# Head forms through eight staging slots, an x-sum loaded later, and a re-timed end of the gated-convolution units, in a streaming hybrid layer

## The chip, the cores and the metric

The kernel runs on one core of one Trainium2 chip. The metric is device time in microseconds (us) of that core. TensorE is called PE here, VectorE DVE, ScalarE ACT, GpSimd POOL and SyncE SP; PEld is PE's loading of weights, which runs beside its matmuls.

## The reference

One layer of a streaming encoder is computed for 512 prompt frames of a new stream and 64 frames of a running one (with 512 cached keys and values). All inputs and outputs are float32.

```
D_MODEL 2048; 8 heads x 128; 8 conv groups x 128 channels, width 3; D_FF 5632; IN_COLS 6144
def hybrid_layer(x, ...):
    hn = rmsnorm(x, g_norm1)
    q, k, v, gb, gc, hc = split(hn @ w_in)            # six times 1024 columns
    q, k = rmsnorm(q, g_q), rmsnorm(k, g_k)           # per head
    o_attn = stick_breaking_blocks(q, k_all, v_all, P).reshape(B, T, 1024)
    u = gc * hc
    conv = conv_w[0]*padded[:, 0:T] + conv_w[1]*padded[:, 1:T+1] + conv_w[2]*padded[:, 2:T+2]
    o_conv = gb * conv                                # padded = past state, then u
    mix = concatenate([rmsnorm(o_attn, g_attn_out), rmsnorm(o_conv, g_conv_out)])
    x = x + mix @ w_out
    h2 = rmsnorm(x, g_norm2)
    x = x + (silu(h2 @ w_gate) * (h2 @ w_up)) @ w_down
```

New keys, values and conv states are outputs too.

## The kernel before

**Layout and precision.** Features lie on the 128 partitions and frames in the free dimension: 512 + 64 = 576 frames, worked in two halves of 288 (`HALVES`). A float32 operand is split into a rounded high part (a cast on ACT, line 223 in `split`) and the remainder as a low part (a subtraction on DVE, or on POOL where `lo_eng` says so, line 224). A product is three matmuls: high by high, low weight by high, high weight by low. One "tick" of the software pipeline `pipe` is one such group of three matmuls; generators that yield a number of ticks are put into the instruction streams between them.

**Stages.** First come norms, q/k/v projections and attention, head by head, then two conv groups in the plain way (`conv_group`, `STD` = 2). The other six conv groups, and the attention half of the output projection, are computed in units of a 2x2 block scheme that needs seven products (numbers 1 to 7, with sums of weights and sums of inputs) in place of eight. There are 17 units: n = 0 to 8 are conv units (lists `CU`, `NCU` = 9; kind "u" makes u = gc * hc of a group, kind "b" the gate of two groups), n = 9 to 16 are output units (kind "o"), one for each 256 output columns. A product of a conv unit has 24 matmuls, one of an output unit 12. After the units comes the plain output projection of the conv half (`out_proj`, bank name `pjo`), which starts at 855.88 us of the profile, then the second norm and the feed-forward part to the end.

**Order of the units.** PE runs the products in a list written out by hand, `corder` (lines 1089 to 1097); `conv_run` issues one product and the work on its bank, and `conv_prepare`, four places ahead in the list, forms the weight sum of a later product on DVE and splits it (`whl`, two tags in turn). The raw columns of w_in and w_out lie in three places, which `call_columns` fills when they fall free: 0 and 1 (`raw_a`, 1 MB each) and 2 (`bt["raw"]`, named `raw_c`); output units use 0 and 1 alone. Except for PE, the order on each engine is the scheduler's; from product 1 of the last conv unit on, SP's too is the order in which the code is written, for as long as `turn_mode` is open (lines 1100 to 1117).

**Inputs of the products.** In a conv unit products 5, 6, 7 and 4 read sums of x blocks. Sum 0 lies in `xt` (loaded by the eight DMAs of line 1085), sums 1, 2 and 3 in tiles `xs_t1` to `xs_t3` of 2.3 MB each (tags t1 to t3), all three loaded in `open_b` when attention ends. Product 6 reads sum 1, product 7 sum 2, product 4 sum 3, product 5 sum 0. In an output unit the seven inputs are "forms" of the normed heads. `head_forms` makes them: a sum of squares over the heads, the row scale `acc_a`, then for each of four head pairs two scalings on DVE, the three forms 1, 2, 3, which are blocks, and four forms 5, 7, 6, 4, which POOL makes by subtraction. `put` splits each into a tile `hf` and stores it to `form_dram` by SP (line 542): 28 forms, 288 KB each. The tile comes from tag "hl" of the pool `tmp`, with two buffers, which `put_mix` and the squares of `group_scale` use as well. `load_forms` fetches the forms into tags t1, t2, t3 and "oa" during the last conv unit (lines 1108 to 1114), as the products that read the old contents end.

**The last conv unit and the output units.** The order of unit 8 is 1, (unit 7's 3 and 4), 6, 7, 5, 4, 2, 3. After product 5 the bank `psw` is read by DVE (`done`, lines 1003 to 1007, name `cv`), and product 4 adds to the same bank. After product 3 `open_out` opens tiles for the residual (16 loads `x` from `xt_dram`, one for each 128 rows, all issued at once on SP) and for `mixc`, the normed conv outputs that `put_mix` had written to `mix_dram`; `load_mix` asks for its two halves at ticks 60 and 120. `group_scale` makes the row scale `R_c` of the conv half: squares split at once, their sums on PE 40 ticks later (`ssg`), `rsqrt_mean` (lines 457 to 466: `ms` on DVE, logarithm and exponential on ACT, three DVE steps with `y` and `t`), then the second half of the frames in the same way 80 ticks after the start. `ms` has one buffer, and `kept("ms")`, the copy of product 1's bank (`part`, line 991), has the same tag. The eight output units hold 8 x 28 = 224 ticks. The first two weights of `out_proj` are loaded at the tenth and fifth product before the end of `corder`.

Of the kernel before, what the change touches and what calls it, by code (L numbers as in the profile page):

```python
# [10 lines left out]
F32 = mybir.dt.float32  # L11
F32R = mybir.dt.float32r
# [4 lines left out]
P = 128  # L17
TP = 512
TS = 64
T = TP + TS  # L20
HALF = T // 2
# [13 lines left out]
NP = KD // 2  # L35
# [59 lines left out]
def tile_hybrid_stream_step(  # L95
# [6 lines left out]
    nc = tc.nc  # L102
# [13 lines left out]
    rpool = ctx.enter_context(tc.tile_pool(name="rpool", bufs=1, side="left"))  # L116
# [92 lines left out]
    pipe = Pipeline()  # L209
# [16 lines left out]
    def parts(name):  # L226
        t = tmp.tile([P, 2, HALF], F32R, tag="hl", name=name)
        return t[:, 0], t[:, 1]
# [290 lines left out]
    def head_forms():  # L519

        two = [parts("sqg") for _ in HALVES]
        for (sh, sl), (a, b) in zip(two, HALVES):
            split(sh, sl, acc_a[:, a:b])
        yield 6
        for (sh, sl), (a, b) in zip(two, HALVES):
            rsqrt_mean(acc_a[:, a:b], channel_sums(sh, sl, a, b, "ssg"), 8 * P, HALF)
        yield 8
        for k in range(NH // 2):  # L530
            pair = o_half[k // 2][:, 2 * (k % 2) : 2 * (k % 2) + 2, :]
            four = pair.rearrange("p k (i t) -> p (k i) t", i=2)
            b11, b12, b21, b22 = (four[:, q, :] for q in range(4))
            for r in range(2):
                nc.vector.scalar_tensor_tensor(out=pair[:, r], in0=pair[:, r], scalar=col("ga", 2 * k + r), in1=acc_a,
                                               op0=ALU.mult, op1=ALU.mult)
            yield 2

            def put(f, src, lo_eng):
                t = tmp.tile([P, 2, HALF], F32R, tag="hl", name="hf")  # L540
                split(t[:, 0], t[:, 1], src, lo_eng)
                nc.sync.dma_start(out=form_dram[f - 1, k].rearrange("f p t -> p f t"), in_=t.bitcast(F32))

            for f, src in ((1, b11), (2, b21), (3, b22)):
                put(f, src, nc.vector)
                yield 2
            for f, out, a, b in ((5, b11, b12, b11), (7, b12, b12, b22), (6, b22, b22, b11), (4, b21, b21, b22)):
                nc.gpsimd.tensor_tensor(out=out, in0=a, in1=b, op=ALU.subtract)
                yield 1
                put(f, out, nc.gpsimd if f in (5, 6) else nc.vector)  # L550
                yield 2

    def group_scale(acc, dst, rows_of):

# [273 lines left out]
    def open_b():  # L828

        pipe.flush()  # L830
        t1.release()
        bt["pool"] = bpool = tc.alloc_tile_pool(name="bpool", bufs=1, reuse_waits="tile", side="left")
        for q in (1, 2, 3):
            t = bt[q] = bpool.tile([P, NP, 2, HALF], F32R, tag=f"t{q}", name=f"xs_t{q}")
            nc.sync.dma_start(out=t.bitcast(F32), in_=xs_dram[q].rearrange("j f p t -> p j f t"))
        bt["acc"] = acon.tile([P, T], F32, tag="ac", name="acc_c")
        pipe.spawn(head_forms(), 2)

    def open_units():
        bt["raw"] = apool.tile([P, 2048], F32, tag="oa", name="raw_c")  # L840
        cx = apool.tile([P, 1024 + UW], F32, tag="ob", name="cx")
        bt["s1"] = cx[:, :1024].rearrange("p (j c) -> p j c", c=P)
        bt["c"] = cx[:, 1024 : 1024 + UW - 2]
# [36 lines left out]
    def conv_group(g):  # L880
        gates = []

        def evac_gc(ps, a, b):
            t = tmp.tile([P, HALF], F32, tag="sq", name="gcr")
            nc.vector.tensor_tensor(out=t, in0=ps, in1=R1[:, a:b], op=ALU.mult)
            nc.vector.tensor_tensor(out=t, in0=t, in1=R1[:, a:b], op=ALU.mult)
            gates.append(t)

        project(evac_gc)
        begin_u(g)  # L890
        project(lambda ps, a, b: put_u(a, b, ps, gates[a // HALF]))

        def evac_gb(ps, a, b):
            if not bt:
                open_b()
            if a == 0:
                end_u(g)
            t = tmp.tile([P, HALF], F32, tag="y", name="gbr")
            nc.vector.tensor_tensor(out=t, in0=ps, in1=R1[:, a:b], op=ALU.mult)
            put_o(g, a // HALF, t)  # L900

        if g == STD - 1:
            call_columns(range(2))
            for p_ in (1, 2):
                conv_prepare(0, p_)
        project(evac_gb)
# [11 lines left out]
    def call_columns(gone):  # L918
        cfree.extend(gone)
        while cwanted:  # L920
            n, c = cwanted[0]
            place = [q for q in cfree if c is not None or q < 2][:1]
            if not place:
                return
            cwanted.pop(0)
            q = place[0]
            cfree.remove(q)
            raw = bt["raw"] if q == 2 else raw_tile["A"][:, q, :]
            if c is None:
                d = CU[n][1]  # L930
                nc.sync.dma_start(out=raw.rearrange("p (k c) -> p k c", c=2 * P),
                                  in_=w_out[:AW, 2 * d * P : 2 * (d + 1) * P].rearrange("(k p) c -> p k c", p=P))
                v = raw.rearrange("p (j s h c) -> p j s h c", s=2, h=2, c=P)
                for c in range(2):
                    cregion[n, c] = q, v[:, :, 0, c, :], v[:, :, 1, c, :]
            else:
                c0 = cstart[c + 2 * (CU[n][0] == "b")] + CU[n][1] * P
                nc.sync.dma_start(out=raw.rearrange("p (k c) -> p k c", c=P),
                                  in_=w_in[:, c0 : c0 + P].rearrange("(k p) c -> p k c", p=P))
                v = raw.rearrange("p (j s c) -> p j s c", s=2, c=P)  # L940
                cregion[n, c] = q, v[:, :, 0, :], v[:, :, 1, :]
# [106 lines left out]
    def open_out():  # L1048

        xpool.release()  # L1050
        bt["y"] = ypool = tc.alloc_tile_pool(name="ypool", bufs=1, reuse_waits="tile", side="right")
        x2t.extend(ypool.tile([P, 2, T], F32, tag=f"y{j}", name=f"x2_{j}") for j in range(NP))
        bt["m"] = tc.alloc_tile_pool(name="mpool", bufs=1, reuse_waits="tile", side="right")
        bt["mc"] = bt["m"].tile([P, 2, NG, 2, HALF], F32R, name="mixc")
        for kt in range(KD):
            nc.sync.dma_start(out=x2(kt), in_=xt_dram[kt])
        bt["R"] = rpool.tile([P, T], F32, tag="R", name="R_c", bufs=2)
        pipe.spawn(state_out())
        pipe.spawn(group_scale(bt["acc"], bt["R"], 40))
        pipe.spawn(load_mix())  # L1060

    def load_mix():
        for i in range(2):
            yield 60
            nc.sync.dma_start(out=bt["mc"][:, i].bitcast(F32), in_=mix_dram[i].rearrange("k f p t -> p k f t"))

    def state_out():
# [17 lines left out]
        nc.sync.dma_start(out=xt[j][:, 0, 1].bitcast(F32), in_=xs_dram[0, j].rearrange("f p t -> p f t"))  # L1085
    pipe.flush()
    open_units()
    call_columns([2])
    corder = [(0, 1), (0, 2), (1, 1), (1, 2), (0, 6), (0, 7), (0, 5), (0, 3), (0, 4), (1, 6), (1, 7), (1, 5)]
    for n in range(2, len(CU)):  # L1090
        if n == NCU - 1:
            corder += [(n, 1), (n - 1, 3), (n - 1, 4), (n, 6), (n, 7), (n, 5), (n, 4), (n, 2), (n, 3)]
        elif n == NCU:
            corder += [(n, p_) for p_ in (1, 2, 6, 7, 5)]
        else:
            corder += [(n, 1), (n - 1, 3), (n - 1, 4), (n, 2), (n, 6), (n, 7), (n, 5)]
# [4 lines left out]
    for k_, (n, p_) in enumerate(corder):  # L1101
        if (n, p_) == (NCU - 1, 1):
            turn_mode.enter_context(tc.manual_schedule(engines={mybir.EngineType.SP}))
        conv_run(n, p_)
        if k_ + 4 < len(corder):
            conv_prepare(*corder[k_ + 4])
        if n == NCU - 1 and p_ in (6, 7, 4):
            q = {6: 1, 7: 2, 4: 3}[p_]
            t = bt["pool"].tile([P, NH, 2, HALF], F32R, tag=f"t{q}", name=f"forms{q}")
            for at, f in enumerate({1: (1, 2), 2: (6, 7), 3: (5, 3)}[q]):  # L1110
                load_forms(t, 4 * at, f)
            if p_ == 7:
                load_forms(apool.tile([P, NH // 2, 2, HALF], F32R, tag="oa", name="forms0"), 0, 4)
        if (n, p_) == (NCU - 1, 3):
            open_out()
            turn_mode.close()
        if k_ in (len(corder) - 10, len(corder) - 5):
            load_weight()
        if k_ == len(corder) - 4:
            split_weight(nc.vector)  # L1120


    ypool, mpool, mc, R_c = (bt[n] for n in ("y", "m", "mc", "R"))
# [616 lines left out]
```

## Time and profile before

| what | value |
|---|---|
| median of 3 runs | 2456.91 us (2456.89 to 2457.04) |
| profiled execution, its own time | 2452.86 us |
| span of the profile | 2451.1 us |
| mean granted clock of PE | 0.99 |
| PE / PEld busy | 2383.6 (97%) / 2368.5 (97%) us |
| DVE / ACT / POOL busy | 1903.9 (78%) / 1168.5 (48%) / 290.4 (12%) us |
| DMA | 386.05 MB, mean 157 GB/s |
| first matmul of the first unit | 504.58 us |
| first matmul of `out_proj` | 855.88 us |

The profile shows one execution. Busy time counts an engine's own work and not its waiting; SP's DMA issues appear as a queue (SPq). In lists of groups and in timelines an entry reads "output<-input", with "L982" for line 982 of the kernel, and in brackets the idle time of the engine before it and what ended that. Times in timelines and windows are us from the start of the span, on which attention and the two plain conv groups end at about 504 us.

### The profile page before, as it was taken

Reading aid. Unit: us, or ns where it says so; the run is one execution under the profiler, and the core shown is the slowest. Engines: PE = TensorE matmul, PEld = TensorE weight load, DVE = VectorE, ACT = ScalarE, POOL = GpSimd, SP = SyncE. Lnnn points to the kernel's source line nnn. Section 1 sums busy time; section 2 is a strip of 40 time slices with the busy share of each in tenths; the row PEclk is TensorE's granted clock in tenths of the full one; section 3 lists DMA queues with packets and bytes.
Section 4 is the critical chain, followed back from the end, with each engine's and each line's share of the span. In section 5 each row is a group of like instructions: output and inputs, shape, how many; then the busy total and the mean of one; then the engine's idle time right before and its main releaser. Section 6 shows DMA issues by size and latency. Waiting matters only on the chain.

```text
span 2451.1 us, 44205 instructions
## 1 busy us (share of the span) xinstructions
PE 2383.6 (97%) x17825; PEld 2368.5 (97%) x17825; DVE 1903.9 (78%) x2862; ACT 1168.5 (48%) x2091; POOL 290.4 (12%) x400
## 2 busy tenths in 40 slices
PE   8999999959998999999999999999999999999999
PEld 8999999949998999999999999999999999999999
DVE  7876666548886766988888888888888777887875
ACT  6766556334443444544444444444444444444454
POOL 1111111131112222000000000000000001431211
PEclk9999999979999999999999999999999999999999
DMA  8564232663339343445344444443444845885542
GB/s 281 162 184 125 86 92 71 214 199 114 118 123 339 94 134 125 126 144 158 114 153 147 146 137 129 152 157 122 148 142 147 294 158 177 252 224 196 194 142 79
DMA packets 504085, 386.05 MB, mean 157 GB/s; under 512 B 11854, under 2 KB 493000, under 8 KB 503880
## 3 DMA queue, kind: packets, MB, share of 16 engines
q1 hardware_dynamic: 496712, 371.40, 47.5%
q0 software_dynamic: 6448, 11.51, 2.1%
q8 instruction: 139, 2.28, 0.4%
q14 instruction: 66, 0.54, 0.1%
q10 hardware_dynamic: 720, 0.33, 0.0%
HBM read 296.47 MB, written 86.72 MB: 156 GB/s over the span
## 4 chain that ended last, share of the span: by engine, by line
PE 64%; DVE 2%; ACT 0%; DMA 0%; issue 0%; ACTq 0%; DVEq 0%
PE psy L1490 32%; PE psw L1490 16%; PE psx L1490 8%; PE pjo L214 4%; PE pw L1333 2%; PE psy L982 1%; DVE whl L224 1%; PE psw L982 0%; PE pot L1647 0%; DMA raw_b<-in_w_gate_dram 0%; DVE raw_a L1439 0%; PE psx L982 0%; DMA hid_dram<-form 0%; DVE s L1435 0%; ACT whl L223 0%
## 5 line engine op out<-in xcount | busy, mean ns | idle before, releaser
L224 DVE TENSOR_TENSOR whl<-raw_a,whl 128x1024 fp32r<-128x1024 f32 (+4 forms) x372 | 391.1, 1052 | 76.7 <-ACT whl L223 75.4
L1490 PE MATMUL psy<-t,whl 128*128 128x288 f32 x2916 | 436.8, 295 | 0.0
L1490 PE MATMUL psy<-h_s,whl 128*128 128x288 f32 x2724 | 410.7, 294 | 1.8 <-ACT part L1500 1.8
L223 ACT CAST whl<-raw_a 128x1024 fp32r<-128x1024 f32 (+4 forms) x372 | 326.8, 881 | 164.4 <-issue 37.0
L1490 PEld LDWEIGHTS psy<-t,whl 128*128 128x128 f32 x2916 | 402.9, 188 | 0.2
L214 PE MATMUL pj<-x,whi 128*128 128x288 f32 x1856 | 397.6, 299 | 0.3 <-DVE x L357 0.3
L1490 PEld LDWEIGHTS psy<-h_s,whl 128*128 128x128 f32 x2724 | 377.4, 188 | 2.3 <-ACT part L1500 2.2
L1490 PE MATMUL psw<-t,whl 128*128 128x288 f32 x2592 | 377.0, 295 | 0.0
L1490 PEld LDWEIGHTS psw<-t,whl 128*128 128x128 f32 x2592 | 353.7, 188 | 0.2
L214 PEld LDWEIGHTS pj<-x,whi 128*128 128x128 f32 x1856 | 306.6, 189 | 1.0 <-DVE x L357 0.6
L214 PE MATMUL pj<-x,wlo 128*128 128x288 f32 x928 | 274.5, 296 | 0.1
L224 DVE TENSOR_TENSOR whl<-raw_b,whl 128x1024 fp32r<-128x1024 f32 (+5 forms) x186 | 194.1, 1044 | 69.4 <-ACT whl L223 68.4
L223 ACT CAST whl<-raw_b 128x1024 fp32r<-128x1024 f32 (+5 forms) x186 | 161.2, 868 | 163.5 <-issue 69.5
L1500 ACT COPY part<-psy 128x288 f32<-128x288 f32 x237 | 94.6, 399 | 269.9 <-PE psy L1490 268.9
L214 PEld LDWEIGHTS pj<-x,wlo 128*128 128x128 f32 x928 | 175.0, 189 | 0.7 <-DVE wlo L424 0.3
L1490 PE MATMUL psx<-h_s,whl 128*128 128x288 f32 x1122 | 164.5, 294 | 0.0
L1490 PEld LDWEIGHTS psx<-h_s,whl 128*128 128x128 f32 x1122 | 154.0, 188 | 0.0
L1253 POOL DMA_DIRECT2D hid_dram<-form x3 | 2.2, 727 | 975.7 <-DVE form L224 973.8
L223 ACT CAST whl<-s 128x1024 fp32r<-128x1024 f32 (+5 forms) x79 | 70.2, 889 | 99.1 <-PE psw L1490 97.6
L982 PE MATMUL psy<-x,whl 128*128 128x288 f32 x648 | 90.4, 299 | 16.2 <-ACT whl L223 15.0
L177 DVE TENSOR_TENSOR wlo<-raw_a,whi 128x1024 fp32r<-128x1024 f32 (+1 forms) x80 | 98.1, 1242 | 10.4 <-ACT whi L176 8.2
L982 PEld LDWEIGHTS psy<-x,whl 128*128 128x128 f32 x648 | 88.3, 192 | 17.2 <-ACT whl L223 15.3
(442 smaller groups left out, 4000.2 us busy)
## 6 DMA issues: line engine op xcount, KB each, us to landing
hid_dram<-form SPq DMA_DIRECT2D x147, 288.0 KB, 2.6
raw_a<-in_w_in_dram SPq DMA_DIRECT2D x41, 1024.0 KB, 5.6
raw_a<-in_w_gate_dram SPq DMA_DIRECT2D x23, 1024.0 KB, 6.0
raw_a<-in_w_up_dram SPq DMA_DIRECT2D x23, 1024.0 KB, 5.4
raw_b<-in_w_gate_dram SPq DMA_DIRECT2D x21, 1024.0 KB, 6.8
raw_b<-in_w_up_dram SPq DMA_DIRECT2D x21, 1024.0 KB, 7.3
h_s<-hid_dram SPq DMA_DIRECT2D x10, 2016.0 KB, 8.7
raw_a<-in_w_out_dram SPq DMA_DIRECT2D x16, 1024.0 KB, 5.2
```

Source lines behind the costliest of these rows:

```text
L177: lo_eng.tensor_tensor(out=lo[:, a:b], in0=raw[:, a:b], in1=hi[:, a:b].bitcast(F32), op=ALU.subtract)
L214: mm(ps, w_[:, k, csl], x_, start=(k == 0 and n == 0), stop=(k == nk - 1 and n == 2))
L223: nc.scalar.copy(out=hi, in_=src)
L224: (lo_eng or nc.vector).tensor_tensor(out=lo, in0=src, in1=hi.bitcast(F32), op=ALU.subtract)
L982: mm(ps, whl[:, w_, j, :], x_, start=(start and j == 0 and q == 0), stop=(j == m - 1 and q == 2), skip_group_check=True)
L1253: q.dma_start(out=hid_dram[fp][2 * n - 2 : 2 * n].rearrange("f p t -> p f t"), in_=t.bitcast(F32))
L1333: mm(pss[j, i], w_[:, k, j * P : (j + 1) * P], x_, start=(kk == 0 and k == 0 and n == 0), stop=(kk == 1 and k == 7 and n == 2))
L1490: mm(ps, whl[:, w_, j, :], x_, start=(start and j == 0 and q == 0), stop=(j == len(xs_) - 1 and q == 2), skip_group_check=True)
L1500: nc.scalar.copy(out=t, in_=st["y"])
```

## The change

It has four parts.

1. `put` in `head_forms` takes its tiles from eight slots in turn (`bt["stage"]`, tag t3, the place that `xs_t3` had held from the start) in place of the two buffers of tag "hl". `open_b` loads x-sums 1 and 2 alone; sum 3 is loaded by `load_sum(3)` at the end of `head_forms`, once the slots are free. The third raw place is opened after the second head pair is done, and `call_columns` asks for all three places in the last plain conv group, in place of asking for the third one after the flush.
2. In the last conv unit product 2 stands ahead of product 4.
3. The residual tiles are loaded two at a time, 11 ticks apart (`load_rest`), and the two loads of `mixc` follow, 20 ticks apart. SP keeps the written order to the end of the list of products: `turn_mode` closes after the loop.
4. `group_scale` starts 7 * 28 = 196 ticks later than before, which is at the start of the last output unit, with 7 ticks in place of 40 between its steps.

```diff
--- before.py
+++ after.py
@@ -520,6 +520,7 @@
 
 
 
+        turn = [0]
         two = [parts("sqg") for _ in HALVES]
         for (sh, sl), (a, b) in zip(two, HALVES):
             split(sh, sl, acc_a[:, a:b])
@@ -537,7 +538,8 @@
             yield 2
 
             def put(f, src, lo_eng):
-                t = tmp.tile([P, 2, HALF], F32R, tag="hl", name="hf")
+                t = bt["stage"][:, turn[0] % NP]
+                turn[0] += 1
                 split(t[:, 0], t[:, 1], src, lo_eng)
                 nc.sync.dma_start(out=form_dram[f - 1, k].rearrange("f p t -> p f t"), in_=t.bitcast(F32))
 
@@ -549,6 +551,9 @@
                 yield 1
                 put(f, out, nc.gpsimd if f in (5, 6) else nc.vector)
                 yield 2
+            if k == 1:
+                bt["raw"] = apool.tile([P, 2048], F32, tag="oa", name="raw_c")
+        load_sum(3)
 
     def group_scale(acc, dst, rows_of):
 
@@ -830,14 +835,17 @@
         pipe.flush()
         t1.release()
         bt["pool"] = bpool = tc.alloc_tile_pool(name="bpool", bufs=1, reuse_waits="tile", side="left")
-        for q in (1, 2, 3):
-            t = bt[q] = bpool.tile([P, NP, 2, HALF], F32R, tag=f"t{q}", name=f"xs_t{q}")
-            nc.sync.dma_start(out=t.bitcast(F32), in_=xs_dram[q].rearrange("j f p t -> p j f t"))
+        bt["stage"] = bpool.tile([P, NP, 2, HALF], F32R, tag="t3", name="hf")
+        for q in (1, 2):
+            load_sum(q)
         bt["acc"] = acon.tile([P, T], F32, tag="ac", name="acc_c")
         pipe.spawn(head_forms(), 2)
 
+    def load_sum(q):
+        t = bt[q] = bt["pool"].tile([P, NP, 2, HALF], F32R, tag=f"t{q}", name=f"xs_t{q}")
+        nc.sync.dma_start(out=t.bitcast(F32), in_=xs_dram[q].rearrange("j f p t -> p j f t"))
+
     def open_units():
-        bt["raw"] = apool.tile([P, 2048], F32, tag="oa", name="raw_c")
         cx = apool.tile([P, 1024 + UW], F32, tag="ob", name="cx")
         bt["s1"] = cx[:, :1024].rearrange("p (j c) -> p j c", c=P)
         bt["c"] = cx[:, 1024 : 1024 + UW - 2]
@@ -900,7 +908,7 @@
             put_o(g, a // HALF, t)
 
         if g == STD - 1:
-            call_columns(range(2))
+            call_columns(range(3))
             for p_ in (1, 2):
                 conv_prepare(0, p_)
         project(evac_gb)
@@ -1052,16 +1060,18 @@
         x2t.extend(ypool.tile([P, 2, T], F32, tag=f"y{j}", name=f"x2_{j}") for j in range(NP))
         bt["m"] = tc.alloc_tile_pool(name="mpool", bufs=1, reuse_waits="tile", side="right")
         bt["mc"] = bt["m"].tile([P, 2, NG, 2, HALF], F32R, name="mixc")
+        bt["R"] = rpool.tile([P, T], F32, tag="R", name="R_c", bufs=2)
+        pipe.spawn(load_rest())
+        pipe.spawn(state_out())
+        pipe.spawn(group_scale(bt["acc"], bt["R"], 7), 7 * 28)
+
+    def load_rest():
         for kt in range(KD):
             nc.sync.dma_start(out=x2(kt), in_=xt_dram[kt])
-        bt["R"] = rpool.tile([P, T], F32, tag="R", name="R_c", bufs=2)
-        pipe.spawn(state_out())
-        pipe.spawn(group_scale(bt["acc"], bt["R"], 40))
-        pipe.spawn(load_mix())
-
-    def load_mix():
+            if kt % 2:
+                yield 11
         for i in range(2):
-            yield 60
+            yield 20
             nc.sync.dma_start(out=bt["mc"][:, i].bitcast(F32), in_=mix_dram[i].rearrange("k f p t -> p k f t"))
 
     def state_out():
@@ -1085,11 +1095,10 @@
         nc.sync.dma_start(out=xt[j][:, 0, 1].bitcast(F32), in_=xs_dram[0, j].rearrange("f p t -> p f t"))
     pipe.flush()
     open_units()
-    call_columns([2])
     corder = [(0, 1), (0, 2), (1, 1), (1, 2), (0, 6), (0, 7), (0, 5), (0, 3), (0, 4), (1, 6), (1, 7), (1, 5)]
     for n in range(2, len(CU)):
         if n == NCU - 1:
-            corder += [(n, 1), (n - 1, 3), (n - 1, 4), (n, 6), (n, 7), (n, 5), (n, 4), (n, 2), (n, 3)]
+            corder += [(n, 1), (n - 1, 3), (n - 1, 4), (n, 6), (n, 7), (n, 5), (n, 2), (n, 4), (n, 3)]
         elif n == NCU:
             corder += [(n, p_) for p_ in (1, 2, 6, 7, 5)]
         else:
@@ -1113,11 +1122,12 @@
                 load_forms(apool.tile([P, NH // 2, 2, HALF], F32R, tag="oa", name="forms0"), 0, 4)
         if (n, p_) == (NCU - 1, 3):
             open_out()
-            turn_mode.close()
         if k_ in (len(corder) - 10, len(corder) - 5):
             load_weight()
         if k_ == len(corder) - 4:
             split_weight(nc.vector)
+
+    turn_mode.close()
 
 
     ypool, mpool, mc, R_c = (bt[n] for n in ("y", "m", "mc", "R"))
```

## The prediction

> **What bounds the kernel now.** First the page's slices. PE is at 9 or more nearly everywhere; there is one 5 and one 8, and the granted clock dips in both. Only there can this change win.
>
> ```profile
> PE   8999999959998999999999999999999999999999
> PEclk9999999979999999999999999999999999999999
> ```
>
> Second, the windows view cut at the matmuls where PE runs without a break on both sides (stretch; length; PE, PEld, DVE, ACT, POOL busy; clock; DMA share; GB/s). The second stretch is full; the others are not.
>
> ```profile
> 504.58:562.71 58.13, 27.99 (x171) 26.65 (x169) 23.40 (x34) 17.53 (x32) 15.89 (x20) 0.71 0.63 198
> 562.71:718.31 155.60, 155.60 (x1177) 155.60 (x1177) 132.47 (x172) 66.81 (x91) 21.44 (x41) 1.00 0.37 112
> 718.31:815.32 97.01, 81.19 (x560) 78.67 (x558) 73.39 (x120) 39.49 (x74) 18.82 (x23) 0.94 0.70 250
> 815.32:855.88 40.56, 39.77 (x288) 39.54 (x289) 30.84 (x44) 17.66 (x33) 9.80 (x10) 0.96 0.34 105
> ```
>
> A full product of a conv unit is 24 matmuls and takes 3.17 us (155.60 / 1177 = 0.132 each). Stretch A, 504.58 to 562.71, holds seven products: 22.2 us of work, so 35.9 are lost. Stretch B, to 815.32, holds seven of 24 and 32 of twelve plus four small ones: 73.7 of work, 23.3 lost. Stretch C, to 855.88, has 288 matmuls: 38.0, 2.5 lost. In all 61.7 us; the stretch from 855.88 to the end is dense already.
>
> Third, the timelines of PE, ACT and SP around A (start, length, what; in brackets the idle time before and what ended it).
>
> ```profile
> 526.12 0.61 PE L982 MATMUL psy<-x,whl 128*128 128x288 f32 x1 [15.04 <-ACT whl L223]
> 548.65 0.61 PE L982 MATMUL psy<-xs_t,whl 128*128 128x288 f32 x1 [12.94 <-ACT whl L223]
> ...
> 541.55 0.43 ACT L223 CAST hf<-o_ob 128x288 fp32r<-128x288 f32 x1 [2.22 <-DMA form_dram<-hf]
> 545.99 1.04 ACT L223 CAST whl<-raw_a 128x1024 fp32r<-128x1024 f32 x1 [0.24 <-DVE raw_a L951]
> ...
> 518.57 0.46 SPq L938 DMA_DIRECT2D raw_c<-in_w_in_dram  x1
> 519.38 24.38 SPq L542 DMA_DIRECT2D form_dram<-hf  x12
> ```
>
> PE waits twice for a weight cast on ACT. ACT is not busy: it stands in its queue behind `hf` casts, and each of these waits for the store of the form two before it to land. So 28 forms take from 469.37 (first cast) to 542.38 (last), 2.6 us each; the cast of unit 0's product 6 comes after them, and the load of `raw_c` can only be issued at 518.57, in the place that the forms leave. The view of waits sums it up:
>
> ```profile
> ACT hf L223 <- DMA form_dram<-hf: 38.8, 23, 5.8
> ```
>
> Fourth, B and C, from PE, SP, DVE and ACT:
>
> ```profile
> 734.98 4.98 PE L982 MATMUL psw<-xs_t,whl 128*128 128x288 f32 x24 [3.12 <-DVE cv L1005]
> 783.55 2.82 PE L982 MATMUL psy<-forms,whl 128*128 128x288 f32 x12 [1.99 <-ACT part L991]
> 815.32 6.35 PE L982 MATMUL psy<-forms,whl 128*128 128x288 f32 x36 [4.30 <-ACT part L991]
> ...
> 747.51 17.68 SPq L1056 DMA_DIRECT2D x<-xt_dram  x16
> 767.10 0.40 SPq L931 DMA_DIRECT2D raw_a<-in_w_out_dram  x1
> ...
> 810.32 0.46 DVE L461 TENSOR_SCALAR ms<-ssg 128x288 f32<-128x288 f32 x1 [0.70 <-POOL x L1001]
> 814.87 0.40 ACT L991 COPY part<-psy 128x288 f32<-128x288 f32 x1 [2.62 <-DVE R_c L466]
> ```
>
> 734.98 is product 4 of the last conv unit: it adds to the bank that DVE has just to read for product 5. 783.55 and 815.32 are the two halves of the row scale: `ms` has one buffer, which `kept` uses too, so the chain ms, y, t, R_c and the part copies wait for each other while PE stands. Sixteen residual loads hold SP for 17.68 us, and the weight load of unit 11 comes after them.
>
> **The change, part by part.**
>
> *Eight form buffers, x-sum 3 later.* No form waits for the landing before last. What paces them next is POOL: per head pair four subtractions and two lower parts at 0.81 (x 6 = 4.9 us), against 7 casts on ACT at 0.43 and 5 lower parts at 0.45 plus two scalings at 0.81 on DVE. Starting at the first subtraction (472.94), three pairs are done by 487.6. But in the changed program's order the two `raw_a` loads and the `raw_c` load of units 0 and 1 stand on SP behind 23 form stores (before: behind two, four and sixteen). I put the 23rd at 493, with 5 us for the other work in DVE's order. A load lands 5.7 us after issue (the DMA view), the next ones 2.7 later each (1 MB at the 390 GB/s of 740 to 780): 498.7, 501.4, 504.1. Cast and split (1.04 + 1.22) make unit 0's first operand ready at 501.0; PE arrives at 504.58: 3.6 us in hand. The second weight of unit 0 and `raw_c` have more. Then the eight x loads and x-sum 3, 4.6 MB or 12 us, which cannot start before the last projection ends and the forms have landed (504.6 to 509): landed by 521. Product 5 of unit 0 reads the first at 523.6, product 4 the second at 529.9. Each wait fits, with 2 to 4 us in hand; if it doesn't, PE pays one for one. Of the 18 POOL operations ahead of the 23rd store some meet DVE at work, and that has a price:
>
> ```profile
> 521.46 0.79 POOL L224 TENSOR_TENSOR hf<-o_ob,hf 128x288 fp32r<-128x288 f32 x1 [0.30 <-ACT hf L223]
> 527.76 1.72 POOL L224 TENSOR_TENSOR hf<-o_ob,hf 128x288 fp32r<-128x288 f32 x1 [5.51 <-ACT hf L223]
> ```
>
> The second ran beside a 1.22 us DVE split, and took 0.93 longer. Six of 18 make 5.6, less 3.6 in hand is 2; with the slow matmuls that follow a gap I leave 3 us in A (bounds 0 and 14.8, below). A gains 32.9.
>
> *Product 2 before product 4.* The bank's chain (end of 5 to start of 4, 3.12 idle) now has product 2, 3.17 us, beside it, with its weights split ahead. The gap and the slow start after it (24 matmuls in 4.82 to the next group, 1.65 over) go: 4.8. Form loads of the third x-sum's place go out one product later, 3.17 us; their reader, product 5 of the first output unit, already waited 1.24, and stays about there since the queue ahead of it is the same.
>
> *Two residual tiles at a time, SP in written order to the end.* Unit 11's weights stand behind six small loads in place of eighteen; the two gaps of 1.51 and 0.59 at 774 and 775 with their slow matmuls, 2.4, go. The later residual tiles come at two per 11 ticks (4.4 us) and are used at two per 28, so none is late; `mixc` is asked for at ticks 108 and 128 of 224. Cost nothing, hidden by that distance.
>
> *Row scale in the last output unit.* The two halves now cost 3.66 (783.55: gap 1.99, then 1.04 and 0.63 over) and 5.73 (815.32: gap 4.30, then 1.43 over): 9.4. The same operations with the same single `ms` buffer remain, now seven ticks apart. Bounds: nothing, if a gap hides in the turn to the output projection, and all 9.4. I take 4, by the nearer row, 3.66, since the second half falls where no further unit's parts compete. 5.4 gained.
>
> *What stays:* of B 23.3 - 4.8 - 2.4 - 8.0 (the part of the row scale before 815.32) = 8.1, the waits for `mix_dram` stores, for forms and for the first residual tile behind 8 MB of forms; of C 1.1.
>
> Left: 3 + 8.1 + 4 + 1.1 = 16.2. Gain 61.7 - 16.2 = 45.5. On the profiled execution 2452.86 - 45.5 = 2407.4; the median of the runs, 2456.91, lies 4.05 above that execution, so 2411.4.
>
> The slow matmuls are in these sums as measured: after a gap of 1.99 us the next twelve took 2.62 instead of 1.59. The Trainium skill (TensorE: Matmul & The Clock Gate, Part 1: The HAM clock gate) says that the clock halves only after about 3.4 us of idleness. By that the gaps left here would have no such tail, and the estimate would be about 2406; the trace shows a tail after shorter gaps, so I keep it.
>
> **Rivals.**
>
> 1. *POOL and DVE block each other.* All 18 POOL operations pay 0.93: 16.7 - 3.6 = 13.1, and 1.65 of slow matmuls: 14.8 in A. Gain 33.7: 2423. For it: the two rows above. Against: POOL waits for others in between, and many 0.81 rows lie beside DVE work. The Trainium skill (SBUF — State Buffer, Who interferes with whom) has it as a lock: a DVE operation with two SBUF inputs and a GpSimd one that reads SBUF wait for each other to the end; the rows above agree.
> 2. *The forms keep their pace* (the eight places act as one, so that landings still count): 2.6 us each, 23rd store at 530, first weights landed at 536, PE stands from 504.58 to 538.3. A gains 1, the rest 12.6: 2443. Against: in the changed order only the ninth and later casts wait for a store.
> 3. *Slower: the weights behind the stores.* The same queue, with forms slower than now, because casts, POOL and stores also meet the 4.6 MB of x-sums. Before, seven products were done at 562.71; they are later than that once product 1 of unit 0 starts after 540.5, and the gains of B and C are gone too once the 23rd store leaves after 545. At 4 us a form it leaves at 561: A loses 31 - 2 more than now, less 12.6: 2473. Against: no row shows a form over 2.7 us that did not wait for a landing or a 2.3 MB load.
>
> **Numbers.** Forecast 0.77, rival 1 0.14, rival 2 0.05, rival 3 0.04. Range: all good bounds (A 0, row scale 0, 8.1 less its slow half) give 55: 2402; rival 1 with the full 9.4 for the row scale gives 28: 2428. Outside lie rivals 2 and 3 and a little. A measurement here tells about 0.2%, 5 us, from no change. Faster 0.94, same 0.02, slower 0.04.
>
> **What would show it.** `hf` casts without waits for `form_dram` and done by 500; no PE gap over 3 us between 504 and 560; the 23rd store at 488 to 497; no wait on `cv` L1013 ahead of product 4; the `ssg` sums near the last unit with one gap of 2 to 4; the output projection starting at 808 to 813 in place of 855.88. Wrong if a PE gap stands on `whl<-raw_a` at 505, or if x loads land after 524.

## The result and the profile after

The changed kernel takes 2414.55 us (median of 4 runs, 2412.46 to 2414.96) against 2456.97 for the kernel before in the same set of runs: a ratio of 0.9825, with a 95% interval of 0.9808 to 0.9842. That is 42.4 us less, 1.7%. The forecast was 2411.4, with 45.5 us of gain.

The page's slices, in the form shown of the kernel before, no longer have a hole:

```profile
PE   8999999999999999999999999999999999999999
...
PEclk9999999999999999999999999999999999999999
```

The profiled execution has 2414.43 us, a span of 2412.7. One thing has to be set right before it is compared. Its last projection ends at 506.56, where the kernel before's ended at 504.74. The two profiles part long ahead of anything that was changed: between 60 and 80 us PE's granted clock is 0.91 in the one and 1.00 in the other. Over all profiles of this study this end lies between 502.1 and 506.6, and the kernel before itself read 2453.5 to 2457.0 in different sets of runs. So times of different kernels are compared here by three stretches of their profiles: **I**, from the end of the last projection to product 7 of unit 2; **II**, from there to the first product of an output unit; **III**, from there to the first matmul of the output projection. Each is the difference of two times in the timeline of PE; differences of stretches given below are taken before rounding.

| kernel (profile) | I | II | III | sum | median us |
|---|---|---|---|---|---|
| before | 89.8 | 151.6 | 109.7 | 351.1 | 2456.97 |
| after | 63.4 | 147.1 | 99.8 | 310.3 | 2414.55 |
| e1 part 1 alone | 63.1 | 150.5 | 113.4 | 327.0 | 2428.97 |
| e2 parts 2 to 4 alone | 90.8 | 146.2 | 102.5 | 339.5 | 2439.76 |
| e3 two slots | 85.1 | 146.4 | 101.6 | 333.2 | 2434.72 |
| e12 four slots | 65.9 | 146.8 | 102.9 | 315.6 | 2415.09 |
| e4 old order of unit 8 | 63.1 | 152.4 | 98.8 | 314.3 | 2413.29 |
| e5 early row scale | 63.5 | 146.3 | 107.0 | 316.8 | 2419.61 |
| e6 sixteen residual loads | 63.2 | 146.6 | 109.7 | 319.5 | 2421.17 |
| e7 first columns early | 60.8 | 146.7 | 101.8 | 309.3 | 2412.34 |
| e8 mix from dead places | 63.1 | 146.5 | 102.4 | 312.0 | 2415.41 |
| e9 and forms 4, 5 exchanged | 62.8 | 146.5 | 102.0 | 311.2 | 2414.47 |
| e10 e7, second columns first | 59.5 | 146.8 | 107.7 | 314.0 | 2414.52 |
| e11 e9 and e10 | 59.7 | 146.7 | 105.5 | 311.9 | 2413.49 |

In the sum the change gained 40.9 us (351.1 - 310.3, rounded); behind it the rest of the kernel is the same to 0.6 us. Four profiles with the same code from unit 2 on (after, e3, e7, e12) have 99.8 to 102.9 in III, 101.5 in the mean; that spread is to be kept in mind where III is compared, and both values are given below. Where the rest of the loss sits is seen in the windows view of the changed kernel, cut again where PE is dense on both sides (columns as in the prediction):

```profile
506.56:547.71 41.15, 35.26 (x240) 33.74 (x241) 30.30 (x38) 15.96 (x21) 4.99 (x7) 0.96 0.81 266
547.71:716.99 169.28, 168.86 (x1275) 168.37 (x1274) 145.96 (x194) 73.33 (x102) 23.47 (x45) 1.00 0.43 132
716.99:735.00 18.01, 13.50 (x87) 12.77 (x85) 10.18 (x20) 7.47 (x17) 3.81 (x5) 0.91 1.06 386
...
803.34:816.83 13.49, 10.61 (x78) 10.14 (x77) 9.70 (x14) 6.75 (x12) 3.09 (x3) 1.00 0.33 101
```

The first row holds ten products of 24 (31.7 us of work at 0.132 each): 9.4 lost. The second holds 53: 1.1 lost. The third holds 84 matmuls (11.1): 6.9 lost, with the DMA engines full. The last holds 72 and four small ones (10.1): 3.4 lost. Together 20.8, where the forecast had 16.2. The waits behind these losses, from the timelines of PE, ACT and SP (a run of slow matmuls behind a gap is called its tail below):

```profile
508.32 0.40 PE L990 MATMUL psy<-x,whl 128*128 128x288 f32 x1 [1.77 <-ACT whl L223]
509.58 4.85 PE L990 MATMUL psy<-x,whl 128*128 128x288 f32 x23 [0.86 <-DVE whl L224]
...
522.14 3.44 PE L990 MATMUL psx<-x,whl 128*128 128x288 f32 x24 [1.33 <-DVE cv L1013]
...
544.57 3.30 PE L990 MATMUL psy<-xs_t,whl 128*128 128x288 f32 x23 [1.15 <-DVE whl L224]
...
722.86 1.87 PE L990 MATMUL psy<-forms,whl 128*128 128x288 f32 x12 [2.43 <-ACT part L999]
...
728.34 6.57 PE L990 MATMUL psy<-forms,whl 128*128 128x288 f32 x36 [1.99 <-ACT part L999]
...
810.92 1.86 PE L990 MATMUL psy<-forms,whl 128*128 128x288 f32 x12 [2.39 <-ACT part L999]
...
503.08 0.43 ACT L223 CAST hf<-o_ob 128x288 fp32r<-128x288 f32 x1 [0.55 <-POOL o_ob L550]
...
719.12 0.54 ACT L513 ACTIVATE mx<-cv,vec 128x288 fp32r<-128x288 f32 x1 [3.92 <-DMA mix_dram<-mx]
...
726.89 0.43 ACT L223 CAST sqg<-acc_c 128x288 fp32r<-128x288 f32 x1 [3.56 <-DMA mix_dram<-mx]
...
474.70 25.79 SPq L544 DMA_DIRECT2D form_dram<-hf  x23
500.54 3.19 SPq L946 DMA_DIRECT2D raw_a<-in_w_in_dram  x2
503.77 3.40 SPq L946 DMA_DIRECT2D raw_c<-in_w_in_dram  x1
...
527.95 6.62 SPq L946 DMA_DIRECT2D raw_a<-in_w_in_dram  x2
```

The last `hf` cast starts at 503.08, the first at 471.20: 28 forms in 32.3 us in place of 73.4, and the view of waits has no row any more in which `hf` waits for `form_dram`. The casts' brackets name POOL now, in 15 waits of 18.2 us in all. On SP the three loads of raw columns stand behind the 23rd store, as the order had said. Two gaps of the start of the output units (722.86 and 728.34) end with ACT's copy `part`, which stood in ACT's queue. Ahead of the first were two scalings of the mix (`mx`, at 719.12 and 721.66) that had waited 3.92 and 1.16 us for a mix store to land; ahead of the second was the cast `sqg` of the row scale, after a wait of 3.56. The code starts `group_scale` 196 ticks later, but in ACT's queue, which the scheduler orders, its first cast is still at 726.89. It too waits for a mix store to land, because `put_mix` has the same two buffers.

### The profile page after: what moved, and what is told of

Its sections match the earlier page's. It is cut to its first block, busy times and chain, and to the rows that moved or that the text cites. A ratio compares the mean times of both kernels' runs of the same rounds, so it can differ in the third digit from the quotient of the medians.

```text
span 2412.7 us, 44204 instructions
## 1 busy us (share of the span) xinstructions
PE 2377.6 (99%) x17825; PEld 2363.1 (98%) x17825; DVE 1910.5 (79%) x2862; ACT 1166.6 (48%) x2091; POOL 294.6 (12%) x400
## 4 chain that ended last, share of the span: by engine, by line
PE 79%; DVE 10%; DMA 5%; ACT 3%; issue 2%; POOL 1%; SPq 0%; ACTq 0%; DVEq 0%; POOLq 0%
PE psy L1500 33%; PE psw L1500 16%; PE pj L214 8%; PE psx L1500 8%; PE pjo L214 4%; DVE whl L224 3%; PE psy L990 2%; DMA raw_a<-in_w_in_dram 2%; PE pw L1343 2%; PE psw L990 1%; DVE wlo L177 1%; PE psx L990 1%; DMA raw_c<-in_w_in_dram 1%; DMA xs_dram<-xs_out 1%; DMA x<-xt_dram 1%
## 5 line engine op out<-in xcount | busy, mean ns | idle before, releaser
L214 PE MATMUL pjo<-mixc,whi 128*128 128x288 f32 x512 | 101.7, 294 | 0.0
L176 ACT CAST whi<-raw_a 128x1024 fp32r<-128x1024 f32 (+1 forms) x85 | 85.6, 1023 | 20.1 <-PE pjo L214 9.0
```

What stands on the lines that cost most here:

```text
L176: nc.scalar.copy(out=hi[:, a:b], in_=raw[:, a:b])
L214: mm(ps, w_[:, k, csl], x_, start=(k == 0 and n == 0), stop=(k == nk - 1 and n == 2))
```

## The experiments

**Do the parts add up?** e1 is the kernel before with part 1 alone, e2 the kernel before with parts 2, 3 and 4 alone (the diffs are the parts of the diff above).

> The kernel before with part 1 alone (eight slots, x-sum 3 later, the raw loads asked for earlier). If the parts add up, this keeps what the changed kernel gained between the last projection and the eleventh product, 35.9 - 9.4 = 26.5 us, and none of the rest: 2457 - 26.5 = 2430.5. If the queue ahead of the last conv unit (forms loads, weights) is moved by part 1 as well, the end of the units gains or loses some 2 us beside it: 2428 to 2433. Rival: the end of the units now pays for what part 1 won (its loads come in a denser stretch): over 2436.

Measured: 2428.97 against 2453.53 of the kernel before in the same set, 24.6 less. The sum of the stretches is 24.2 less: 26.7 in I, as expected, 1.1 in II, but 3.7 given back in III.

> The kernel before with parts 2, 3 and 4 (product 2 ahead of 4, residual tiles two at a time, row scale late) and not part 1. By the forecast's terms 12.6 us less: 2444. By the changed kernel's trace, in which the last conv unit and the output units lost 1.1 + 6.9 + 3.4 = 11.4 where the kernel before lost 25.8, 14.4 less: 2442.5. Rival: the first output unit's waits stand where part 2 won (the gap ahead of product 4 moves behind the weights' casts): 2447 or more.

Measured: 2439.76 (its own runs spread from 2434.6 to 2442.3) against 2453.53, 13.8 less, between the two forecasts of 12.6 and 14.4; the stretches give 11.6. By the stretches the two make 35.8 and the whole change 40.9: together they are worth 5 us more than apart. The difference is in III, where the two alone gain 3.6 in sum and the whole change 9.9. From the timelines of SP and PE of e1:

```profile
738.85 0.40 SPq L939 DMA_DIRECT2D raw_a<-in_w_out_dram  x1
...
745.89 0.46 PE L990 MATMUL psy<-forms,whl 128*128 128x288 f32 x1 [4.01 <-ACT whl L223]
```

With sixteen residual loads ahead of it on SP, the weight load of unit 11 was issued 22.3 us after the first output product (738.85, product at 716.59; in the kernel before 21.0), and PE waited 4.01 for it, where the kernel before, which came there later after its start of the output units, waited 1.51. So PE does pay there for a part of what part 1 won, as the rival of e1 says, but not at its price: 24.6 less than 2457 is 2432.4, within the 2428 to 2433 of the second case and not over 2436.

**The slots.** In the code only the number of slots differs; where the loads of raw columns stand on SP is the scheduler's, and that differs too.

```diff
-                t = bt["stage"][:, turn[0] % NP]
+                t = bt["stage"][:, turn[0] % 2]      # e3; % 4 in e12
```

> The changed kernel, but the forms go out by two of the eight slots in turn (x-sum 3 still comes last). Theory: the forms are paced by the landing of the store two before; then their casts take 2.3 to 2.7 us each again in place of 1.14 (32 us for 28), some 65 to 73 us in all, the first seven products end 45 to 58 us after the last projection in place of 29, and the time is 2431 to 2445. Rival: what held them was the load of x-sum 3, 2.3 MB, on the same queue; then the forms stay near 1.2 us each and the time is within 4 us of 2414.5.

> The changed kernel with four of the eight slots. With two slots the 28 casts took 68.5 us (2.52 each), with eight 32.3 (1.18). Theory: a slot is held from its cast to the landing of its store, some 1 us of work and 2.2 to 4.75 us of landing in the changed kernel's trace, 3.2 to 5.8 in all; over four slots that is 0.8 to 1.45 us a form, about the pace that POOL sets anyway, so four do nearly what eight do: casts in 32 to 40 us, the stretch from the last projection to the third unit's product 7 61 to 66 us (eight: 63.4; two: 85.1), the time within 3 us of 2414.5. Rival: half the slots, half the gain, because landings grow with the stores in flight or POOL and DVE wait for the same slots: casts near 50 us, the stretch 72 to 76, the time 2422 to 2426.

From the views of waits of e3 and e12 (us in total, times, longest):

```profile
ACT hf L223 <- DMA form_dram<-hf: 42.3, 23, 6.9
...
ACT hf L223 <- DMA form_dram<-hf: 18.9, 16, 6.0
```

With two slots the old wait is back whole (38.8 in the kernel before), 28 casts take 68.5 us, and I is 85.1: 21.7 of the 26.4 us that I had gained are lost. PE's two holes are back, 7.43 and 15.75 us, both ended by a cast of weights on ACT. x-sum 3 still comes last there, so it was not that load which held the forms. With four slots the casts take 46.7 us and still wait 18.9; the rival's pace, near 50, was right and the theory's 32 to 40 was not. Yet I is only 65.9, since the scheduler put the first load of raw columns behind 4 stores instead of 23 in this kernel. So with four slots the forms still wait for landings, and PE hardly pays for it because the load has moved as well. What four slots give with the load behind 23 stores, and what five to seven give, no run shows.

**The loads behind the stores.** e7 asks for unit 0's first columns one projection earlier; e10 also loads unit 1's first columns ahead of unit 0's second.

```diff
         project(evac_gc)
         begin_u(g)
+        if g == STD - 1:
+            call_columns([0])
         project(lambda ps, a, b: put_u(a, b, ps, gates[a // HALF]))
...
-            call_columns(range(3))
+            call_columns([1, 2])
...
-    cwanted = [(n, c) for n in range(NCU) for c in range(2)] + ...
+    cwanted = [(0, 0), (1, 0), (0, 1), (1, 1)] + [(n, c) for n in range(2, NCU) for c in range(2)] + ...   # e10
```

> The changed kernel with the load of unit 0's first raw columns asked for one projection earlier; on SP it then stands behind 12 form stores in place of 23, so it is issued near 485 to 493 in place of 500.5. Theory: the first two gaps of the units (1.77 and 0.86) and the slow matmuls behind them (1.9) come from this load alone: 3 to 4.5 us less, 2410 to 2411.5, with the gap of 1.33 ahead of unit 1's second product left or moved earlier. Rival: the next load (the second raw columns, or raw_c) or DVE's queue of splits is late next by as much: within 1.5 us of 2414.5.

> As the kernel with the early load of unit 0's first raw columns (the stretch from the last projection to the third unit's product 7 fell from 63.1 or 63.4 to 60.8 us there, with one gap of 4.42 left, ahead of unit 1's first product), but unit 1's first columns now take the second raw_a place and are loaded ahead of unit 0's second columns. Theory: that gap is the landing of the third load on the queue; as the second it lands 3 us earlier: the gap shrinks to 0 to 2, the stretch is 56 to 58.5 us, and the time 2 to 4.5 us under the early load's 2412.3. Rival: DVE's work behind the loads (two splits and three sums, 6 us in a row) is what PE waits for; then the wait comes back ahead of unit 0's product 6 and the stretch stays over 59.5.

PE's timeline of e7, then of e10:

```profile
516.64 4.84 PE L992 MATMUL psy<-x,whl 128*128 128x288 f32 x23 [4.42 <-DVE whl L224]
...
512.53 3.35 PE L992 MATMUL psy<-x,whl 128*128 128x288 f32 x23 [1.27 <-DVE whl L224]
...
517.40 3.47 PE L992 MATMUL psx<-x,whl 128*128 128x288 f32 x24 [1.53 <-DVE cv L1015]
```

In e7 unit 0 starts without a wait, and all smaller waits of I but one of 0.49 become one of 4.42, ahead of unit 1's first product, whose columns (`raw_c`) are the third load. PE does not wait there for their landing: ACT's casts of them begin at 510.46, but DVE takes four sums of unit 0's columns first and begins the split at 515.36. I falls by 2.6, where 3 to 4.5 were expected. In e10 that gap is 1.27, and I falls by 3.9; what is left names DVE (1.27 and 1.53), whose splits and sums of three operands stand in one row. A later gap of 1.16, ahead of unit 1's product 6, is another matter: there DVE has stood idle for 5.29 us until the fourth load landed. The rival of e10 (DVE's queue) has the rest: I stays at 59.5, its bound. The time of e7 is 2412.34 (2410.59 to 2415.37), 2.2 us below the changed kernel's, but the kernel before read 3.4 lower in that set too: no gain that can be told. In e10 III is 7.8 longer than in the changed kernel: the loads for the output units took other places, and in SP's written order the second of two such loads, waiting for its place, held the forms until 701.38, 9.7 us ahead of the first product that reads one. In the changed kernel they leave at 700.97, 16.0 us ahead.

**Product 2 ahead of product 4.** e4 undoes part 2 alone.

> The changed kernel with the last conv unit's old order, product 4 ahead of 2. By the forecast 4.8 us more: 2419.4, with a gap of 3.1 ahead of product 4 again. Rival: the order moved the wait and did not remove it (the gaps of 2.43 and 1.99 in the first output unit, where ACT's queue waits for the stores of the mix, are new); then these gaps shrink to the 1.0 to 1.2 of the kernel before and the time is 1 to 2 us more, 2415.5 to 2416.5.

```profile
707.24 6.01 PE L990 MATMUL psw<-xs_t,whl 128*128 128x288 f32 x24 [3.15 <-DVE cv L1013]
```

The gap ahead of product 4 is back, with a slow tail (6.01 in place of 3.3), and II is 5.3 longer. III is 98.8, so 1.1 shorter than in the changed kernel's profile and 2.7 shorter than the mean. The order is worth 4.2 by the one and 2.6 by the other: both the forecast (4.8) and the rival (1 to 2) have a part of it, since the output units give some of the gain back. Of this worth 2.5 us are the tail, and e1 has the same gap of 3.15 with hardly a tail (24 matmuls in 3.46). The times show no worth at all: e4 took 2413.29 (2411.25 to 2415.50), 1.3 less than the changed kernel, in a set in which the kernel before read 3.4 lower. That the gap goes with the new order is shown; that the time falls by it is not.

**The residual loads and the row scale.** e6 undoes part 3 (and with it SP's written order from there on, and the ticks of the mix loads); e5 undoes part 4.

> The changed kernel with sixteen residual loads at once and the two mix loads at ticks 60 and 120, and SP in the scheduler's order from there. By the forecast 2.4 us more, 2417, with gaps of some 2 us in sum ahead of the products of unit 11. Rival: SP's scheduler moves the weight load ahead or the weights wait in no gap: within 1 us.

> The changed kernel with the row scale early again (start at once, steps of 40 ticks). The late row scale cost 3.4 us in the changed kernel's trace (two gaps of 2.39 and 0.49 with what follows them), the early one 9.4 before: 6 us more, 2420.5, with gaps of 2 and 4 us ahead of the products that stand beside the sums. Rival: the early chain cost so much only because it met the sixteen residual loads; then 1 to 3 us more, 2416 to 2417.

SP's and PE's timelines of e6, then PE's of e5:

```profile
738.41 0.40 SPq L939 DMA_DIRECT2D raw_a<-in_w_out_dram  x1
...
745.38 6.16 PE L990 MATMUL psy<-forms,whl 128*128 128x288 f32 x24 [4.66 <-ACT whl L223]
...
778.94 7.80 PE L990 MATMUL psy<-forms,whl 128*128 128x288 f32 x36 [4.31 <-ACT part L999]
```

Without part 3 the weights of unit 11 leave 24.8 us after the first output product (713.62); before it was 21.0. The queue of forms and residual tiles ahead of them has moved later, which fits the new order of unit 8 (e1, with the old one, had 22.3), and PE is no longer late: it stands 4.66 us, and with the tail III is 9.8 longer (8.2 against the mean), against 2.4 in the forecast. Without part 4 III is 7.2 longer (5.5 against the mean); the gap of 4.30 is there again as 4.31, beside one of 2.22. The forecast's 5.4 was near. By the times, each against the kernel before of its own set, e6 gains 10.0 and e5 8.4 less than the changed kernel.

**The start of the output units.** e8 sends the last mix stores from x places that no product reads any more; e9 also exchanges forms 4 and 5 in their places, so that form 5, read first, is loaded earlier.

```diff
-        t = tmp.tile([P, 2, HALF], F32R, tag="hl", name="mx")
+        if g >= NG - 2:
+            t = xt[4 + 2 * (g % 2) + i][:, 0, 0]
+        else:
+            t = tmp.tile([P, 2, HALF], F32R, tag="hl", name="mx")
...
-            for at, f in enumerate({1: (1, 2), 2: (6, 7), 3: (5, 3)}[q]):        # e9
+            for at, f in enumerate({1: (1, 2), 2: (6, 7), 3: (4, 3)}[q]):
...
-                load_forms(apool.tile(..., tag="oa", name="forms0"), 0, 4)
+                load_forms(apool.tile(..., tag="oa", name="forms0"), 0, 5)
```

> The changed kernel, but the four stores of the last conv unit's mix leave from four dead places of x in place of the two buffers of tag hl. Theory: the first output unit loses its 6.9 us because ACT's queue stands behind a cast of the mix, and one of the row scale's squares, that wait for a mix store to land (3.92, 1.16 and 3.56 us of ACT's idle time); without that the gaps of 2.43 and 1.99 go, with their slow matmuls: 4.5 to 6 us less, 2408.5 to 2410. Rival: the next one late is the load of forms or the first residual tile, issued at 714 to 721 behind them: 0 to 2 us less.

> The changed kernel with the mix stores from dead places of x (as in the run before this one, where PE then stood 6.00 us for a load of forms), and with forms 4 and 5 exchanged in their places: form 5, the fifth to be read, is loaded behind product 7, and form 4 behind product 4. Theory: the order with product 2 ahead of 4 moves the load of form 5 one product later, and that, not the mix, is the later of two waits at the start of the output units; with both away the stretch from the first output unit to the output projection falls from 99.9 (102.4 with the mix stores alone) to 94 to 96 us, and the time by some 4 to 6 us, 2409 to 2411. Rival: the weights of unit 10 or the first residual tile are next, and the stretch stays over 98.5.

PE's timeline of e8, then of e9, and two windows of e9:

```profile
727.07 6.52 PE L993 MATMUL psy<-forms,whl 128*128 128x288 f32 x36 [6.00 <-DMA forms<-form_dram]
...
724.08 3.41 PE L993 MATMUL psy<-forms,whl 128*128 128x288 f32 x24 [1.72 <-DMA forms<-form_dram]
...
731.15 3.12 PE L993 MATMUL psy<-forms,whl 128*128 128x288 f32 x12 [3.67 <-DMA forms<-form_dram]
...
720.00:725.00 5.00, 3.28 (x25) 3.08 (x24) 4.37 (x8) 2.35 (x6) 0.40 (x1) 1.00 1.07 394
725.00:730.00 5.00, 2.49 (x19) 2.26 (x18) 1.99 (x3) 1.54 (x3) 0.00 (x0) 1.00 1.08 393
```

Both theories fell. e8 takes ACT's waits away, as its theory says, and PE waits 6.00 for form 5 instead, as its rival has it. e9 brings form 5 earlier: PE still waits 1.72 for it, and then 3.67 for form 3, which is loaded last. So the rival of e9 was right in the stretch (over 98.5), though what came next was another form and not weights or a residual tile. III does not move: 102.4 and 102.0, at a mean of 101.5 without the edits. The DMA engines are full (1.07, 394 GB/s) at that time: seven loads of forms of 1.2 MB, weights and residual tiles come in one row, and whichever the order, one of them is late. As far as these two edits show, the 6.9 us there are a matter of bytes and of when their places fall free, and not of buffers.

> The changed kernel with the early load, unit 1's columns second, the mix stores from dead places and forms 4 and 5 exchanged. The two stretches do not touch, so the gains should add up: from the last projection to the output projection 310.3 us less 5 to 7 and less 4 to 6, about 298 to 301, and the time 2401 to 2406. If either of the two theories falls, 2406 to 2411.

Measured: 2413.49, 0.9826 of the kernel before, which is over both ranges. I gains 3.7, and III loses 5.7 in the way told of e10, so that all three together are no better than the changed kernel.

## Why the prediction was right, and where it was not

**Right.** The sign, the mechanism of part 1 and most of its size: the forms' casts lose their wait for landings (e3 brings it back), and I falls by 26.4. The wait ahead of product 4 is gone, as forecast; its worth, forecast as 4.8, is 2.6 to 4.2 in e4's profile and does not show in e4's times. Row scale: 4 us left forecast, 3.4 found, with a gap of 2.39 (2 to 4 forecast). What stays elsewhere: 8.1 and 1.1 forecast, in the stretches B and C; 6.9 found at the start of the output units and 1.1 in the conv units ahead of them, with other waits in front. POOL met by DVE: the 18 POOL operations ahead of the 23rd store took 19.17 us where 18 x 0.81 is 14.6, so 4.6 over, with 5.6 forecast (how much of it is DVE's doing no run separates), and the 23rd store left at 500.03: 498.6 by the forecast's terms, plus the 1.8 by which this profile is late.

**Wrong: the 3 us left in A, which are 9.4.** The step that failed is "the second weight of unit 0 and `raw_c` have more" in hand; the sum put nothing for any load behind the first. The first operand itself costs 4.5, where 3 was left: PE waits 1.77 for its cast and 0.86 for its split, 2.6 where 2 was forecast, and the tail is 1.9 where 1 was. Its load landed 6.7 us after issue in place of 5.7. The other 4.9 come behind it.

- `raw_c` left SP at 503.77 and landed at 513.15; its split follows two splits and three sums of the other two loads, and from 508.30 to 524 DVE's timeline shows no idle time. In this row stands the reading of a bank that PE needs for unit 1's product 2: the gap of 1.33, 1.6 with what follows.
- The gaps of 0.28 and 1.15 ahead of unit 1's product 6, 2.1 with their tail, stand at a fourth load, unit 1's second columns. It left SP at 527.95, right behind x-sum 3 and six x loads, and took 9.69 us to land. In e7 the x loads had left some 5 us earlier; there it left at 527.06, landed in 5.51, and neither gap is there.
- A gap of 0.49 behind a copy on ACT, a stall of 0.18 at the last x tile and what follows them make up the other 1.2.

The prediction compared landings and products one by one. It left out the work that loads which come late together release on DVE, and what they cost each other on the way. With the first load moved away (e7) one gap of 4.42 stands at DVE's queue, and with unit 1's columns loaded second (e10) two smaller ones stand there. This is rival 1's place at two thirds of its size, reached mostly by another way. Of the 4.6 us by which the sum of the stretches missed the forecast (45.5 - 40.9) this term has 6.4, and the others gave some back.

**Wrong: part 3 at 2.4.** Its price was read from a gap of the kernel before, in which PE came late for other reasons. Undone in the faster kernel it costs 8 to 10 (e6). The total did not suffer, since the sum goes by what remains, but as the worth of one edit the number was three to four times too small.

**The marks.** Three marks of success came late: the 23rd store at 500.03 (488 to 497 forecast), the end of the casts at 503.5 (500) and the output projection at 816.83 (808 to 813); 1.8 us of each is the late profile, and the rest is not. Both marks of failure are there. The gap of 1.77 stands on the cast of `whl<-raw_a`, but at the size that the sum itself had left for it, so this mark was at odds with the sum. And the prediction named loads of x landing after 524: the last six were issued from 519.63 on, behind the load of x-sum 3 that landed at 528.67, so they all land after it. PE was 8 us later there than forecast (523.6), and product 5 of unit 0 came at 531.76 and found no wait but a stall of 0.18 ahead of its last x tile; the harm fell on the fourth load behind them.

**Luck.** The profiled execution was forecast at 2407.4 and took 2414.43, 7.0 more: 4.6 in the stretches, 1.8 ahead of them and 0.6 behind. The median came out within 3.2 us because the forecast added the 4.05 by which the kernel before's median lay above its profile, and the changed kernel's lies 0.1 above. The 3.4 of the row scale are partly luck too: behind the same gap the ten other profiles with the late row scale have a tail of 0.6 to 1.4 us that this one has not.

**Rivals.** "The forms keep their pace" is what two slots do (e3: 22.9 us in the sum of stretches); eight do not act as one. "The weights behind the stores" had the place right (the raw loads do stand behind 23 stores) and the price wrong, because the forms ran at 1.2 us each and not at 4.

## What to carry to other kernels

Size a staging buffer by the time from its first write to the landing of its store, divided by the pace of the producers: here two slots gave 2.5 us a form, four 1.7 and eight 1.2, where POOL and DVE set the pace. Take the landing from a stretch in which the other loads run: by landings of 2.2 to 4.75 us four slots should have been enough, but with loads of raw columns under way one store of e12 took 7.21 us to land, and a cast waited 6.0 us for another. When loads are held back by a queue, add up the work that all of them release on one engine, not each landing alone. And a gap in a profile prices a wait only for the PE that arrives there now: before a wait is called small, ask how late it is for a PE that comes earlier; one removed wait (ACT behind a mix store) is worth nothing when the next (8 MB of forms on full DMA engines) ends at the same time.

## What the runs showed of the hardware that was not expected

The slow matmuls after a gap come or stay away for the same gap. Ahead of the same product of the last output unit PE idles 2.38 or 2.39 us in the changed kernel, e7 and e9; the twelve matmuls that follow take 1.86 us in the changed kernel, 3.18 in e7 and 3.19 in e9. The granted clock over these twelve matmuls is 1.00 in the changed kernel and 0.53 in e7 and e9. So a tail of 1.3 us is there in two of these three profiles, without a difference in the code at that place, and single profiles differ by that much at one gap. In the eight other profiles that have this gap, of 2.38 to 2.40 us, the twelve take 2.50 to 3.25. The Trainium skill (TensorE: Matmul & The Clock Gate, Part 1: The HAM clock gate) says that the clock is judged in a free-running window of about 3.4 us, which fits a tail that depends on where the gap falls; that a whole window of idleness is needed does not fit, as these gaps are shorter.
